# Storing x in the output and adding the gated product there by accumulating DMAs, in a hybrid-layer kernel on one core

## The chip, the cores and the metric

One core of a Trainium2 chip runs the whole kernel. The metric is the device time of one execution in microseconds; the time of a kernel is the median of its runs.

## The reference

One encoder layer over 2048 prompt tokens and 64 sample tokens (2112 in all), model width 1024, all in fp32. Cut to what matters here:

```python
proj = rms_norm(x, g_pre) @ w_in            # ten groups of 1024 columns
...                                         # path A: gated short convolution; path B: gated linear recurrence, 8 heads
merged = sigmoid(gA) * yA + sigmoid(gB) * yB
x = x + rms_norm(merged @ w_o, g_post)
gate = sigmoid(rms_norm(x, g_ple) @ w_ple_gate)
x = x + (p @ w_ple_proj) * gate             # the output y
```

The change concerns the last line: y is the sum of x (after the second last addition) and the product of the gate with what the text calls p, the projected per-layer embedding.

## The kernel before

The tokens are cut in three ranges ("blocks") of 768, 704 and 640. All data are feature-major: a tile is 128 features by the tokens of a range. Matrix products run in fp32 accuracy by splitting each operand into a high and a low part (three matmuls for each product, lines 388 to 390, 522 to 524 and 558 to 560), and in pairs of column groups by a seven-product scheme (Strassen and Winograd) over half-ranges. Weights come by DMA as tiles of 256 KB: the raw block (line 210), and, where it was computed earlier, its low part (line 232); ScalarE makes the high part (line 231, or 200 where the low part is computed anew on VectorE).

Each range goes through gates, heads (path B), convolution (path A), the merge with W_A and W_B, the product with W_O, a final norm, and the last gate with W_G. The order is written out by hand: generators are advanced at fixed places, `hooks` run one step after each group of matmuls, `paced` makes a POOL DMA wait for a given matmul, and `in_turn` walks over stages of seven steps (n = 0 to 6) with four groups (g = 0 to 3) each. The Tile scheduler then keeps the order of each engine and puts in the semaphores.

Where the last gate of each range is done:

- First range: its gate is a stage of the second range's merge, between W_A and W_B (`merge_in_turn`, `gate_in_turn`).
- Second range: its gate runs in the last range's time, as plain products (`final_gate`), while the last range's norm is done in hooks.
- Last range: its gate is the last stage of all (`gate_in_turn`).

For the first two ranges `final_norm` writes x (after the addition of the normed product) to a spill in HBM, `kept["x", j]` (lines 1225 and 1226), and the input of the gate to `kept["h2", j]`. The product p was written to `kept["p", j]` at the start. When the gate is done, x and p are read back: in the first range's gate `fetch` takes one ring tile for each of 16 half tiles (j, h), x in its left half and p in its right (lines 1161 to 1165), at the groups listed in `FETCH_AT`; in the second range's gate `final_gate` reads x and p for the next j ahead (line 1241, by `reload`, line 1126). Then ScalarE makes the sigmoid (lines 1273 and 1249), VectorE multiplies by p (1274 and 1250) and adds x (1275 and 1251), and the sum is stored to y: by POOL in the first range's gate (line 1277), by SP in the second's (line 1252).

Two pools of tiles matter: `ring` has 50 tiles of one range's width (`rt`), and `hf` has nine tiles of half a range (lines 132 and 133). A tile is given out again when all that read it are done, a store by DMA included. POOL issues its DMAs in order, and also does the power instruction of each norm (line 584).

Of the kernel before, what the change touches and what calls it, by code (L numbers as in the profile page):

```python
# [15 lines left out]
ALU = mybir.AluOpType  # L16
# [3 lines left out]
P = 128  # L20
D = 1024
KB = D // P
# [70 lines left out]
def hybrid_step(  # L93
# [17 lines left out]
    V, A, G, T, SP = nc.vector, nc.scalar, nc.gpsimd, nc.tensor, nc.sync  # L111
    blocks = plan()
# [16 lines left out]
    def rt(n=MAXN + 2, dt=F32):  # L129
        return ring.tile([P, MAXN + 2], dt, tag="r", name=nm("r"))[:, :n]  # L130
# [4 lines left out]
    def wide(x):  # L135
        return x.shape[1]
# [7 lines left out]
    def spill(kind, j, n):  # L144
        return dram.tile([P, MAXN], F32, tag=f"{kind}{j}", name=nm(kind), bufs=2)[:, :n]
# [106 lines left out]
    last, hooks, copies, adds = [None], [], [None], [None]  # L252
# [5 lines left out]
    def paced(dma):  # L258

        tc.add_manual_dep(  # L260
            dma.ins, last[0].name, mybir.DependencyInfo(mybir.DependencyClass.Sync, mybir.DependencyReason.DATA), reason="paced"
        )
# [156 lines left out]
    def half(t, h):  # L419
        n = wide(t) // 2  # L420
        return t[:, h * n : (h + 1) * n]
# [702 lines left out]
    def reload(d, pace=False):  # L1124
        t = rt(wide(d))
        dma = G.dma_start(t, d)
        if pace:
            paced(dma)
        return t

    def merge_in_turn(a, kept, mg, before):

        ob, m = [], []

        def gated(v, x, y):
            V.tensor_tensor(v, whole(x, y), v, ALU.mult)

        def sink_a(g, c, h, x, y):
            gated(half(m[g + c * KH], h), x, y)

        def sink_b(g, c, h, x, y):
            j = g + c * KH
            gated(half(mg[j], h), x, y)
            V.tensor_tensor(half(mg[j], h), half(mg[j], h), half(m[j], h), ALU.add)

        stages = [
            dict(idx=W_A, raw=a, sink=sink_a, anew=("A11", "A12")),
            dict(idx=W_B, raw=ob, sink=sink_b, anew=("A11", "A12")),
        ]
        plan = {(W_A, -1): (kept, GA, m), (W_A, 1): (kept, GA, m), (W_A, 6): (kept, GB, mg), (W_B, 1): (kept, GB, mg)}  # L1150
        if before is None:
            plan |= {(W_A, 3): (kept, "o", ob), (W_A, 5): (kept, "o", ob)}
            order = []
        else:
            rows, fetched = [], {}
            stages.insert(1, gate_in_turn(before[0], rows, lambda j, h: fetched.pop((j, h)), ("A11", "A12", "A22")))
            plan |= {(W_A, 3): (before[1], "h2", rows), (W_A, 5): (before[1], "h2", rows)}
            plan |= {(W_A, 4): (kept, "o", ob), (W_A, 6): (kept, "o", ob), (W_G, 6): (kept, GB, mg)}
            order = [(g + c * KH, h) for c, h in ((0, 0), (1, 0), (1, 1), (0, 1)) for g in range(KH)]

        def fetch(j, h):
            t = rt(before[0]["n"])
            for q, kind in enumerate("xp"):
                paced(G.dma_start(half(t, q), half(before[1][kind, j], h)))
            fetched[j, h] = half(t, 0), half(t, 1)

        def loads(idx, n, g=0, count=1):

            src, kind, tiles = plan.get((idx, n), (kept, None, m))
            if kind is not None:  # L1170
                tiles.extend(reload(src[kind, j], n >= 0) for j in range(len(tiles), len(tiles) + count))
            if idx == W_G and order and n * KH + g in FETCH_AT:
                fetch(*order.pop(0))

        return stages, loads
# [18 lines left out]
    def final_norm(bl, segs, xo, acc, h2, kept, raw=False):  # L1194


        c = slice(segs[0]["off"], segs[-1]["off"] + segs[-1]["n"])
        n = sum(sg["n"] for sg in segs)
        acc2, rs, rs2 = rt(bl["n"]), rt(bl["n"]), rt(bl["n"])
        xks = []  # L1200

        def fetch():
            j = len(xks)
            if j < KB:
                xks.append(rt(bl["n"]))
                G.dma_start(xks[j][:, c], x_fm[j * P : (j + 1) * P, segs[0]["t0"] : segs[0]["t0"] + n])

        fetch()
        copy = V.tensor_copy if bl["last"] else A.copy
        for _ in rms(acc, rs, segs, copy):  # L1210
            fetch()
            yield
        for j in range(KB):
            fetch()
            xj = xo[j][:, c]
            V.scalar_tensor_tensor(xj, xj, g_post[:, j : j + 1], rs[:, c], ALU.mult, ALU.mult)
            V.tensor_tensor(xj, xj, xks[j][:, c], ALU.add)
            for i in (j - 1,) if 0 < j < KB - 1 else (j - 1, j) if j else ():
                sum_squares(i, xo[i][:, c], acc2[:, c], n)
            yield  # L1220
        yield from rms(acc2, rs2, segs, copy)
        for j in range(KB):
            xj = xo[j][:, c]
            if kept is not None:
                kept["x", j] = spill("x", j, bl["n"])
                G.dma_start(kept["x", j], xo[j])
            if len(h2) <= j:
                h2.append(rt(bl["n"]) if raw else (rt(bl["n"], F32R), rt(bl["n"], F32R)))
            t = h2[j] if raw else rt(bl["n"])
            V.scalar_tensor_tensor(t[:, c], xj, g_ple[:, j : j + 1], rs2[:, c], ALU.mult, ALU.mult)  # L1230
            if not raw:
                split(t[:, c], h2[j][0][:, c], h2[j][1][:, c])
            elif kept is not None:
                kept["h2", j] = spill("h2", j, bl["n"])
                G.dma_start(kept["h2", j], t)
                h2[j] = None
            yield

    def final_gate(bl, segs, h2, kept, queue=G):
        def fetch(j):  # L1240
            return [reload(kept[kind, j]) for kind in "xp"] if j < KB else None

        nxt = fetch(0)
        for j in range(KB):
            pss = gemm(W_G + j, h2, segs)
            (xj, pj), nxt = nxt, fetch(j + 1)
            t = rt(bl["n"])
            for s, ps in zip(segs, pss):
                A.activation(t[:, cols_of(s)], ps, AF.Sigmoid)
            V.tensor_tensor(t, pj, t, ALU.mult)  # L1250
            V.tensor_tensor(t, t, xj, ALU.add)
            queue.dma_start(y_fm[j * P : (j + 1) * P, bl["t0"] : bl["t0"] + bl["n"]], t)
            yield

    def rows_again(kept, h2):
# [7 lines left out]
                split(lo.bitcast(F32), hi, lo)  # L1263
                yield

    def gate_in_turn(bl, h2, parts, anew=()):

        def sink(g, c, h, x, y):
            j = g + c * KH
            v = whole(x, y)  # L1270
            gate = hf(wide(v)) if y is None else v
            xj, pj = parts(j, h)
            A.activation(gate, v, AF.Sigmoid)  # L1273
            V.tensor_tensor(gate, gate, pj, ALU.mult)  # L1274
            V.tensor_tensor(gate, gate, xj, ALU.add)  # L1275
            o = bl["t0"] + h * wide(v)
            (SP if (c, h) == (0, 1) and bl["last"] else G).dma_start(y_fm[j * P : (j + 1) * P, o : o + wide(v)], gate)

        return dict(idx=W_G, raw=h2, sink=sink, anew=anew)

# [14 lines left out]
    kepts = [{} for _ in blocks]  # L1295
# [3 lines left out]
    with tc.high_priority():  # L1299
# [41 lines left out]
        ph, done = split_p(ph0)  # L1341
        with behind_all(done):
            done = [held_split(j) for j in range(2)][-1]
# [12 lines left out]
    for n, ks in enumerate(((0,), (1, 2), (3, 4), (5,), (6,), (7,))):  # L1356
        with behind_all(done):
            for k in ks:
                done = add_square(k)
        with placed():  # L1360
            run(first_ple, 1)
        with behind_all(done):
            done = held_split(n + 2)
    with behind_all((*done, *copies)):
        cols = [col_rstd(half(acc, h), n0 // 2) for h in range(2)]
        ph, done = split_p(ph1)
# [26 lines left out]
    for bi, bl in enumerate(blocks):  # L1393
# [57 lines left out]
        if nxt:  # L1451
            fills = gates(nxt, hc, kepts[bi + 1], False)
            norm = final_norm(bl, segs, xo, acc[0], h2, kept, True)
            spread_out((norm, (0, 1, 0, 0, 0, 1) + (0, 1, 0) * (KB - 1) + (0, 1) + (0, 0, 1, 0, 0, 0, 1) + (0, 1) * (KB - 3) + (1, 1, 1)))
            run(fills, LEAD)
            assert not hooks
        else:
            plans = (0, 2, 1, 1, 0, 1, 2, 2, 2, 2), (1, 0, 1, 1, 2, 1, 2, 2, 1, 0, 1, 2, 2, 2, 2)
            spread_out((norms[1], plans[1]), (norms[0], plans[0]))
            raws = load_p(bl, G)  # L1460
            for j, _ in enumerate(final_gate(blocks[bi - 1], blocks[bi - 1]["segs"], rows2, kepts[bi - 1], SP)):
                if j == 3:
                    ph = [split_rt(raw) for raw in raws]
            run(ple(bl, ph, kept))
            assert not hooks
            first_rows = [narrow(half(t, 0)) for t in h2[:KH]]
            run(in_turn([gate_in_turn(bl, h2, lambda j, h: (half(xo[j], h), half(kept["p", j], h)))], first_rows))
# [49 lines left out]
```

## Time and profile before

| | us |
|---|---|
| median of 3 runs | 2552.84 |
| lowest and highest run | 2550.76, 2552.87 |
| the profiled execution, its own time | 2552.61 |
| its span, first to last instruction | 2550.6 |
| VectorE, ScalarE, POOL busy | 1915.9, 1618.7, 421.3 |
| DMA moved | 693.54 MB, mean 272 GB/s |

A busy time is the sum over an engine's instructions in the span; DMA-issuing instructions are not counted on SP, but the time that POOL spends on issuing a DMA (about 0.54 us) is shown where its rows are listed. Rows of a stretch of time give, for each engine, busy us and the number of instructions, then the granted TensorE clock, the mean busy share of the 16 DMA engines and what they moved. A wait is shown as the waiting instruction, what ended the wait, the total, the number and the longest. Rows of single instructions have start and duration in us, the line, what is written and read, and in brackets how long the engine had been idle and what released it. Rows of a line give durations in ns (least, median, largest) and the first and last start. Rows of DMA issues give count, KB each and the median us to landing.

### The profile page before, as it was taken

How to read it: one execution, taken by the hardware profiler on the slowest of the kernel's cores; microseconds unless marked ns; L12 is line 12 of the kernel's file. 1: busy time of each engine (PE TensorE's matmuls, PEld its weight loads, DVE VectorE, ACT ScalarE, POOL GpSimd, SP SyncE). 2: the span in 40 equal slices, each digit the busy share in tenths (PEclk: the TensorE clock that was granted, in tenths of full speed). 3: DMA queues.
4: the chain of work that ended last, by engine and by line, in shares of the span. 5: the costliest groups of instructions: out<-in, count | busy, mean ns of one | idle time of the engine just before them, and what ended most of it. 6: DMA issues, size and time to landing. Idle time of an engine off the chain costs nothing. (4 is left out here: it accounts for less than half of the span.)

```text
span 2550.6 us, 47470 instructions
## 1 busy us (share of the span) xinstructions
PE 2534.3 (99%) x16198; PEld 2519.8 (99%) x16198; DVE 1915.9 (75%) x3714; ACT 1618.7 (63%) x3136; POOL 421.3 (17%) x774
## 2 busy tenths in 40 slices
PE   8999999999999999999999999999999999999999
PEld 8999999999999999999999999999999999999998
DVE  8788888899889867677755578986566655568966
ACT  6666666555465766777845466676677754456736
POOL 1012111222110021223221013102100010011221
PEclk9999999999999999999999999999999999999999
DMA  7678877898888797778777789989866667789977
GB/s 275 217 262 272 279 247 266 288 325 299 283 322 266 255 355 262 246 259 270 252 263 230 212 309 358 338 277 360 307 197 199 196 209 235 234 288 338 312 262 250
DMA packets 330290, 693.54 MB, mean 272 GB/s; under 512 B 41632, under 2 KB 46272, under 8 KB 330048
## 3 DMA queue, kind: packets, MB, share of 16 engines
q1 hardware_dynamic: 283392, 513.73, 60.8%
q0 software_dynamic: 46368, 176.74, 19.2%
q8 instruction: 127, 2.08, 0.3%
q14 instruction: 115, 0.94, 0.1%
q10 hardware_dynamic: 288, 0.05, 0.0%
HBM read 507.10 MB, written 183.26 MB: 271 GB/s over the span
## 5 line engine op out<-in xcount | busy, mean ns | idle before, releaser
L388 PE MATMUL pg<-r,hi 128*128 128x320 f32 (+2 forms) x3304 | 1086.7, 329 | 0.0
L389 PE MATMUL pg<-r,hi 128*128 128x320 f32 (+2 forms) x3304 | 1065.9, 323 | 0.0
L390 PE MATMUL pg<-r,lo 128*128 128x384 f32 (+2 forms) x2056 | 673.0, 327 | 0.0
L388 PEld LDWEIGHTS pg<-r,hi 128*128 128x128 f32 x3304 | 621.6, 188 | 0.4
L389 PEld LDWEIGHTS pg<-r,hi 128*128 128x128 f32 x3304 | 621.4, 188 | 0.0
L231 ACT CAST hi<-raw 128x512 fp32r<-128x512 f32 x544 | 335.3, 619 | 319.2 <-PE pg L389 133.9
L200 ACT CAST hi<-raw 128x512 fp32r<-128x512 f32 x454 | 280.9, 620 | 279.3 <-PE pg L389 132.5
L200 DVE TENSOR_TENSOR lo<-raw,hi 128x512 fp32r<-128x512 f32 x454 | 312.0, 688 | 154.3 <-ACT hi L200 126.1
L523 PE MATMUL pg<-r,hi 128*128 128x384 f32 (+2 forms) x1232 | 398.1, 325 | 1.1 <-DVE r L200 0.6
L390 PE MATMUL pg<-r,s 128*128 128x320 f32 (+1 forms) x1248 | 393.9, 316 | 0.1
L522 PE MATMUL pg<-r,hi 128*128 128x384 f32 (+2 forms) x1232 | 388.2, 325 | 1.1 <-ACT r L200 1.1
L390 PEld LDWEIGHTS pg<-r,lo 128*128 128x128 f32 x2056 | 386.2, 188 | 0.0
L200 DVE TENSOR_TENSOR r<-r,r 128x320 fp32r<-128x320 f32 (+6 forms) x426 | 246.4, 596 | 66.4 <-ACT r L200 64.0
L524 PE MATMUL pg<-r,lo 128*128 128x384 f32 (+2 forms) x800 | 257.8, 324 | 0.9 <-DMA lo<-low 0.9
L523 PEld LDWEIGHTS pg<-r,hi 128*128 128x128 f32 x1232 | 231.3, 188 | 5.9 <-DVE r L200 4.7
L200 ACT CAST r<-r 128x320 fp32r<-128x320 f32 (+6 forms) x426 | 221.0, 547 | 24.9 <-DVE r L369 16.2
L390 PEld LDWEIGHTS pg<-r,s 128*128 128x128 f32 x1248 | 234.4, 188 | 0.3 <-DMA s<-low 0.3
L522 PEld LDWEIGHTS pg<-r,hi 128*128 128x128 f32 x1232 | 228.5, 188 | 5.7 <-ACT r L200 5.0
L200 ACT CAST hi<-s 128x512 fp32r<-128x512 f32 x160 | 98.7, 617 | 113.1 <-PE pg L389 102.5
L402 ACT COPY hf<-pg 128x352 f32<-128x352 f32 (+2 forms) x354 | 156.0, 444 | 10.5 <-PE pg L390 10.3
L524 PEld LDWEIGHTS pg<-r,lo 128*128 128x128 f32 x800 | 150.2, 188 | 1.6 <-DMA lo<-low 1.5
L524 PE MATMUL pg<-r,s 128*128 128x320 f32 (+2 forms) x432 | 139.1, 322 | 0.0
(370 smaller groups left out, 3720.3 us busy)
## 6 DMA issues: line engine op xcount, KB each, us to landing
raw<-w_blk SPq DMA_DIRECT2D x550, 256.0 KB, 4.0
raw<-S SPq DMA_DIRECT2D x488, 256.0 KB, 3.8
s<-low SPq DMA_DIRECT2D x428, 256.0 KB, 3.9
low<-lo SPq DMA_DIRECT2D x178, 256.0 KB, 3.3
S<-s SPq DMA_DIRECT2D x152, 256.0 KB, 3.4
lo<-low SPq DMA_DIRECT2D x116, 256.0 KB, 5.0
low<-r POOLq DMA_DIRECT2D x88, 256.0 KB, 4.8
r<-w_blk POOLq DMA_DIRECT2D x72, 256.0 KB, 7.1
```

The costliest lines, as they stand in the source:

```text
L200: return A.copy(hi, src).ins, V.tensor_tensor(lo, src, hi.bitcast(F32), ALU.subtract).ins
L231: A.copy(hi, raw)
L388: add(hi[:, k, :], xhi, start=start and k == 0, stop=False)
L389: add(hi[:, k, :], xlo, start=False, stop=False)
L390: last[0] = add(lo[:, k, :], xhi, start=False, stop=k == KH - 1).ins
L402: copied = A.copy(got[n], ps[bank])
L522: add(hi[:, k, :], xhi, start=start and k == 0, stop=False)
L523: add(hi[:, k, :], xlo, start=False, stop=False)
L524: last[0] = add(lo[:, k, :], xhi, start=False, stop=k == KH - 1).ins
```

## The change

`final_norm` stores x of the first two ranges straight into y by a plain DMA on POOL (it wrote the spill before) and keeps that instruction. In the two gates p alone is requested: in the first range's gate two halves share one ring tile. The gate times p is then added to y in HBM by an accumulating DMA from POOL (`add_to_y`), which has a semaphore wait on the store of x. The additions on VectorE and the reads of x go; the second range's stores move from SP to POOL. The last range's gate is as before.

```diff
+    def add_to_y(bl, kept, j, o, t):
+
+        done = G.dma_start(y_fm[j * P : (j + 1) * P, bl["t0"] + o : bl["t0"] + o + wide(t)], t, accum_op=ALU.add)
+        tc.add_manual_dep(
+            done.ins, kept["y", j].name, mybir.DependencyInfo(mybir.DependencyClass.Sync, mybir.DependencyReason.DATA), reason="x in y"
+        )
+
     def merge_in_turn(a, kept, mg, before):
...
-            rows, fetched = [], {}
-            stages.insert(1, gate_in_turn(before[0], rows, lambda j, h: fetched.pop((j, h)), ("A11", "A12", "A22")))
+            rows, fetched, shared = [], {}, [None]
+            stages.insert(1, gate_in_turn(before[0], rows, lambda j, h: (None, fetched.pop((j, h))), ("A11", "A12", "A22"), before[1]))
...
         def fetch(j, h):
-            t = rt(before[0]["n"])
-            for q, kind in enumerate("xp"):
-                paced(G.dma_start(half(t, q), half(before[1][kind, j], h)))
-            fetched[j, h] = half(t, 0), half(t, 1)
+            if j % 2 == 0:
+                shared[0] = rt(before[0]["n"])
+            fetched[j, h] = half(shared[0], j % 2)
+            paced(G.dma_start(fetched[j, h], half(before[1]["p", j], h)))
...
             if kept is not None:
-                kept["x", j] = spill("x", j, bl["n"])
-                G.dma_start(kept["x", j], xo[j])
+                kept["y", j] = G.dma_start(y_fm[j * P : (j + 1) * P, bl["t0"] : bl["t0"] + bl["n"]], xo[j]).ins
...
-    def final_gate(bl, segs, h2, kept, queue=G):
+    def final_gate(bl, segs, h2, kept):
         def fetch(j):
-            return [reload(kept[kind, j]) for kind in "xp"] if j < KB else None
+            return reload(kept["p", j]) if j < KB else None
...
-            (xj, pj), nxt = nxt, fetch(j + 1)
+            pj, nxt = nxt, fetch(j + 1)
...
             V.tensor_tensor(t, pj, t, ALU.mult)
-            V.tensor_tensor(t, t, xj, ALU.add)
-            queue.dma_start(y_fm[j * P : (j + 1) * P, bl["t0"] : bl["t0"] + bl["n"]], t)
+            add_to_y(bl, kept, j, 0, t)
...
-    def gate_in_turn(bl, h2, parts, anew=()):
+    def gate_in_turn(bl, h2, parts, anew=(), kept=None):
...
             V.tensor_tensor(gate, gate, pj, ALU.mult)
+            if kept is not None:
+                add_to_y(bl, kept, j, h * wide(v), gate)
+                return
             V.tensor_tensor(gate, gate, xj, ALU.add)
...
```

More of the change, by code (lines that the diff above doesn't have):

```diff
@@ L1274, in sink @@
             V.tensor_tensor(gate, gate, pj, ALU.mult)
+            if kept is not None:
+                add_to_y(bl, kept, j, h * wide(v), gate)
+                return
             V.tensor_tensor(gate, gate, xj, ALU.add)
             o = bl["t0"] + h * wide(v)
-            (SP if (c, h) == (0, 1) and bl["last"] else G).dma_start(y_fm[j * P : (j + 1) * P, o : o + wide(v)], gate)
+            (SP if (c, h) == (0, 1) else G).dma_start(y_fm[j * P : (j + 1) * P, o : o + wide(v)], gate)
         return dict(idx=W_G, raw=h2, sink=sink, anew=anew)
@@ L1460, in hybrid_step @@
             raws = load_p(bl, G)
-            for j, _ in enumerate(final_gate(blocks[bi - 1], blocks[bi - 1]["segs"], rows2, kepts[bi - 1], SP)):
+            for j, _ in enumerate(final_gate(blocks[bi - 1], blocks[bi - 1]["segs"], rows2, kepts[bi - 1])):
                 if j == 3:
```

## The prediction

> **What bounds the kernel now.** I read the page's busy times first, then the waits of TensorE, then the busy time by stage around the places the change touches. All terms below are made against the profiled execution, 2552.61 us, whose span is 2550.6 us; 2.0 us lie around the span. The median of the three runs shown, 2552.84, is 0.2 us above it and the lowest run 1.9 us below, so 0.2% (5.1 us) is about what a measurement can tell from no change.
>
> ```profile
> span 2550.6 us, 47470 instructions
> PE 2534.3 (99%) x16198; PEld 2519.8 (99%) x16198; DVE 1915.9 (75%) x3714; ACT 1618.7 (63%) x3136; POOL 421.3 (17%) x774
> ...
> 6.87 0.69 PE L1103 MATMUL pa<-r,r 128*128 128x384 f32 x1 [6.87 <-ACT r L200]
> ...
> 2544.58 0.31 PE L524 MATMUL pg<-r,lo 128*128 128x320 f32 x1
> ...
> PE pa L1103 <- ACT r L200: 6.9, 1, 6.9
> PE pg L522 <- ACT r L200: 1.1, 1, 1.1
> PE pg L524 <- DMA lo<-low: 0.9, 1, 0.9
> PE pg L523 <- DVE r L200: 0.6, 1, 0.6
> PE pg L459 <- ACT r L767: 0.3, 1, 0.3
> PE pa L1105 <- DVE r L200: 0.2, 1, 0.2
> ```
>
> TensorE is idle for 2550.6 - 2534.3 = 16.3 us only. 6.9 us are the wait for the first input, which nothing here moves. The last matmul starts at 2544.58 and takes 0.31, so 5.7 us follow it (the last gate, its add and its store). Three waits, 1.1 + 0.9 + 0.6 = 2.6 us, remain as something a change in the middle could take away. The next view says where they lie: busy time of each engine in five stretches, then the DMA share and GB/s.
>
> ```profile
> 1543.00:1568.00 25.00, 24.37 (x137) 23.26 (x136) 22.32 (x47) 15.46 (x31) 7.00 (x14) 1.00 0.95 341
> 1568.00:1600.00 32.00, 31.98 (x183) 31.44 (x182) 25.49 (x51) 22.03 (x48) 16.55 (x31) 1.00 1.00 362
> 1600.00:1620.00 20.00, 18.93 (x113) 18.21 (x112) 18.43 (x39) 12.83 (x27) 7.46 (x14) 1.00 1.02 385
> 1620.00:1640.00 20.00, 19.11 (x118) 18.62 (x116) 15.90 (x36) 11.51 (x26) 0.60 (x2) 1.00 0.87 289
> 2414.00:2484.00 70.00, 70.00 (x446) 69.86 (x445) 48.88 (x98) 28.60 (x63) 16.21 (x27) 1.00 0.78 277
> ```
>
> From 1543 to 1620 us runs the gate of the first token range inside the second range's merge (here called the gate stage), and all three waits lie in it or just behind. Its DMA engines are full: 0.95 x 25 + 1.00 x 32 + 1.02 x 20 = 76.2 of 77 us. From 2414 to 2484 the second range's gate runs (the late gate): 78% of DMA, and TensorE never stops. The waits one by one:
>
> ```profile
> 1554.86 0.44 PE L523 MATMUL pg<-r,hi 128*128 128x384 f32 x1 [0.63 <-DVE r L200]
> ...
> 1611.88 0.62 ACT L200 CAST hi<-raw 128x512 fp32r<-128x512 f32 x1 [1.83 <-DMA raw<-w_blk]
> ...
> 1613.29 0.59 PE L522 MATMUL pg<-r,hi 128*128 128x352 f32 x2 [1.07 <-ACT r L200]
> ...
> 1625.79 0.43 PE L524 MATMUL pg<-r,lo 128*128 128x352 f32 x1 [0.89 <-DMA lo<-low]
> ```
>
> The wait at 1613 names ScalarE, but ScalarE had itself stood 1.83 us for a weight; the one at 1625 is a weight's low part. So two of the three (2.0 us) are DMA being late, and the one at 1554 is VectorE, ahead of any add that the change removes. **What decides is therefore DMA time in the gate stage**, not the instructions saved.
>
> **The change part by part.**
>
> ```profile
> L1164 POOL DMA_DIRECT2D r<-x x12: 536/536/550, 1568.0 to 1594.1; - x12
> ...
> L1277 POOL DMA_DIRECT2D y_fm<-hf x16: 539/544/549, 1559.8 to 1612.2; - x16
> ...
> L1277 POOL DMA_DIRECT2D y_fm<-hf x7: 539/544/544, 1583.8 to 1598.6; - x7
> ...
> L1277 POOL DMA_DIRECT2D y_fm<-hf x5: 539/539/544, 1602.7 to 1612.2; - x5
> ...
> q0 software_dynamic: 3823, 12.72, 43.9%
> ...
> r<-x POOLq DMA_DIRECT2D x16, 192.0 KB, 5.5
> ...
> y_fm<-hf POOLq DMA_DIRECT2D x16, 192.0 KB, 5.7
> ...
> y_fm<-hf SPq DMA_DIRECT2D x4, 160.0 KB, 1.8
> ```
>
> (The queue row and the two transfer rows under it are of 1543 to 1620 us alone; the last row is of the kernel's end.) It gives the price of a byte: 43.9% of 77 us is 33.8 us for 12.72 MB, 2.66 us per MB on all 16 engines. A 192 KB transfer (0.197 MB) is 0.52 us of DMA time.
>
> 1. *The x reloads of the gate stage go*: 16 x 0.52 = 8.4 us of DMA time, 16 x 0.54 = 8.6 us of POOL's issuing. The p requests stay, with their pacing, two halves in one tile now. POOL loses only work; its free time between issues is idle already (16.55 of 32 us busy in the fullest stretch), so this half gives nothing.
>
> 2. *The 16 stores of the gate stage become accumulating ones.* Nothing of before shows such a transfer. From below it is a plain store, 0.52 us and 5.7 us to landing. The nearest rows above are the pair it replaces: one x read and one y store move the same bytes over the same engines, 1.04 us, with 5.5 + 5.7 = 11.2 us if one must land before the other. Farther off: if every engine also stood for the shortest store's landing (1.8 us, the last row), 2.84 us each. I take 1.04, because the addend in y must still be fetched from HBM and the sum written: the same read and write, no longer by two instructions. Then DMA time comes out as 16 x 1.04 - 16 x 0.52 - 16 x 0.52 = 0. Ends: -8.4 us and +16 x 1.8 = +29 us.
>
> The Trainium skill, "Collectives: The Full Stack", section "The bandwidth ceiling: the fold count and why AG ≠ RS ≠ AR", speaks against hoping for the low end: an adding transfer is held to half a copy's rate not by the add but by its two source reads on one ring. By that the 16 cost 16.6 us instead of 8.4 and the sum is again 0; no run here shows it yet.
>
> 3. *Where the DMA time falls moves.* Of the 16 x reads four lie before 1568 and 12 in 1568 to 1600; of the stores 4, 7 and 5 in the three stretches. At 1.04 each: 0 before 1568, (7 - 12) x 0.52 = -2.6 us in the second stretch, +5 x 0.52 = +2.6 us in the third, which is the one at 1.02 where weights are late now. What it costs TensorE lies between 0 (the relief just before carries over) and 2.6 us; I take 1.0.
>
> 4. *Adds go.* 16 in the gate stage, 8 in the late gate:
>
> ```profile
> 1558.38 0.56 DVE L1275 TENSOR_TENSOR hf<-hf,r 128x384 f32<-128x384 f32 x1
> ...
> L1251 DVE TENSOR_TENSOR r<-r,r x8: 883/888/894, 2428.0 to 2482.2; 128x704 f32<-128x704 f32 x8
> ```
>
> 16 x 0.56 = 9.0 us and 8 x 0.89 = 7.1 us of VectorE. In the third stretch VectorE is 92% busy (18.43 of 20), so operands for the next stage get ready sooner by up to the 5 adds there, 2.8 us; but the stops there wait for weights. I credit 0.5 us. In the late gate TensorE does not wait, so 0.
>
> 5. *The late gate.* 8 x reads go, 8 stores move from SP to POOL and accumulate.
>
> ```profile
> r<-x POOLq DMA_DIRECT2D x8, 352.0 KB, 6.4
> ...
> L1252 SPq EVENT_SEMAPHORE  x8: 17/2018/2612, 2426.4 to 2483.2; - x8
> L1252 SPq DMA_DIRECT2D y_fm<-r x8: 337/338/655, 2428.9 to 2483.2; - x8
> ...
> 2457.95 0.89 DVE L1250 TENSOR_TENSOR r<-r,r 128x704 f32<-128x704 f32 x1 [3.74 <-ACT r L1249]
> ...
> 2465.76 0.89 DVE L1250 TENSOR_TENSOR r<-r,r 128x704 f32<-128x704 f32 x1 [0.19 <-ACT r L1249]
> ```
>
> SP no longer stands some 2.0 us per store ahead of weight requests: worth 0, since no weight is late there. POOL gets 8 issues of 0.54 us in place of 8 reads of 0.54 us, and now waits for the multiply of line 1250; queued behind it is the p request two groups on, whose multiply comes 2 x 7.8 us later and whose data land in about 6 us, and the norm's power instructions, which follow the same multiply on VectorE anyway. DMA: 0 at the pair's price; if each cost 2.84 us per 192 KB, 8 x 1.8 x 352/192 = 26 us more against 0.22 x 70 = 15 us free, only there could it show. Cover: the free 15 us.
>
> 6. *The x spills (lines 1225 and 1226) become plain stores into y*, 16 of the same size on the same queue: 0. *The new wait for them* is on POOL; they were issued hundreds of microseconds before: 0.
>
> ```profile
> L1226 POOL DMA_DIRECT2D x<-r x16: 539/539/547, 898.1 to 1767.1; - x16
> ```
>
> 7. *Staging tiles.* A gate half (pool hf, nine deep) is held until its store lands. The second store of its group at 1586.46 lands about 5.7 us later; the ninth tile after it is written at 1595.71:
>
> ```profile
> 1586.46 0.54 POOL L1277 DMA_DIRECT2D y_fm<-hf  x1
> ...
> 1595.71 0.47 ACT L544 COPY hf<-pg 128x384 f32<-128x384 f32 x1
> ```
>
> The slack is 3.5 us, so landings up to 9.2 us hide behind it; past that a ScalarE copy, with weight casts queued behind it and TensorE behind those, is late.
>
> Sum: 0 (DMA total) + 1.0 (its place) - 0.5 (VectorE) = +0.5 us: 2553.1 us.
>
> **The rivals.** (a) *The accumulate costs as a plain store.* The stage then has 8.4 us of free DMA, the two weight waits go (-2.0), all three at best (-2.6): 2550.0 to 2550.6. For it: no row excludes it. Against: the bytes of y must be read. Still within 0.2%; a gain over 5.1 us would need more idle time than the 2.6 us there is. (b) *The accumulate makes a third pass*: read, add, write with the engine held, 3 x 0.52 = 1.56 us. 16 x 0.52 = 8.4 us more DMA time where 0.8 of 77 us are free, so TensorE waits for weights about 7.6 us more, from 1583 on: 2560.2. It decides for slower from (5.1 + 0.8)/16 + 1.04 = 1.4 us each. For it: the stage is full, and the landing of weights there is already long:
>
> ```profile
> raw<-S SPq DMA_DIRECT2D x23, 256.0 KB, 7.3
> raw<-w_blk SPq DMA_DIRECT2D x14, 256.0 KB, 10.1
> ```
>
> Against: relief of the x reads just ahead. (c) *Long landing at a fair price*: engine time 1.04, but 11.2 us or more to landing; the tiles of step 7 come 2 us late each, four stores in a row of them, 2 to 8 us on TensorE: 2558. Against: the ninth-tile slack begins at the stores of 1583 only, and ScalarE works ahead. (d) *It is hidden altogether*, -0.5 to 0: the same as the forecast's own range.
>
> **How the numbers follow.** Forecast with (d) 0.65, (a) 0.12, (b) and dearer 0.14, (c) 0.05, something that gains over 5.1 us and that I do not see 0.04. Forecast, (d) and (a) are within 0.2%: 0.77. Slower 0.14 + 0.05 = 0.19, faster 0.04. The likeliest's own range is 2551.5 to 2555.5. The range asked for goes down to (a) less the runs' scatter, 2549.3, and up to (b), 2560.5; what is left out is the dearer part of (b), and the gain.
>
> **What would show it.** Right: no x rows at lines of the fetch, DMA share from 1568 to 1600 a little under 1.00 and from 1600 to 1620 still full, the weight waits near 1613 and 1625 there and up to 1 us longer, the late gate at 70 of 70 us. Rival (a): those two waits gone, GB/s down. Rival (b): more "DMA" waits of TensorE between 1583 and 1640, the gate stage some 7 us longer. Rival (c): waits of ScalarE or VectorE for a DMA into y ahead of tile hf. It would be wrong as a whole if the tail behind the last matmul (5.7 us) changed, which no step touches.

## The result, and the profile after

| | before | changed |
|---|---|---|
| median of 22 runs, us | 2552.27 | 2557.3 |
| ratio, 95% interval | | 1.0018, 1.0011 to 1.0024 |
| profiled execution, its own time (span), us | 2552.61 (2550.6) | 2558.56 (2556.9) |
| VectorE busy, us (instructions) | 1915.9 (3714) | 1902.1 (3690) |

The changed kernel is slower by 0.18%, some 4.6 us, clear of no difference but within the 0.2% that the prediction called no change. In a second measurement it was 1.0018 again (1.0009 to 1.0027). One of the 22 runs of the changed kernel took 14296 us; the ratio leaves it out, and nothing on record says where that time went.

The waits of TensorE in the profile after (total, number, longest):

```profile
PE pa L1103 <- ACT r L200: 6.9, 1, 6.9
PE pg L524 <- DMA lo<-low: 3.4, 1, 3.4
PE pg L390 <- DMA s<-low: 1.0, 2, 0.8
PE pg L522 <- ACT r L200: 0.9, 2, 0.8
PE pg L523 <- DVE r L200: 0.4, 1, 0.4
```

The wait for a weight's low part (line 524) has grown from 0.9 to 3.4 us. The same stretches as before, busy times of each engine, granted clock, DMA share and GB/s, and then the place of the stop (where TensorE stands), first after, then before:

```profile
1543.00:1568.00 25.00, 24.65 (x140) 23.93 (x140) 21.49 (x45) 16.55 (x34) 7.28 (x11) 1.00 1.01 315
1568.00:1600.00 32.00, 32.00 (x184) 32.00 (x183) 22.50 (x45) 21.33 (x46) 12.41 (x19) 1.00 0.97 303
1600.00:1620.00 20.00, 19.10 (x115) 18.50 (x114) 18.69 (x41) 12.11 (x27) 8.54 (x13) 1.00 1.09 329
1620.00:1640.00 20.00, 16.62 (x88) 16.34 (x87) 12.31 (x27) 8.80 (x19) 0.54 (x1) 0.83 0.88 308
...
1621.00:1625.60 4.60, 1.33 (x9) 1.04 (x7) 3.40 (x8) 2.94 (x7) 0.40 (x1) 0.87 1.04 397
1625.60:1632.20 6.60, 6.50 (x25) 6.50 (x26) 2.54 (x4) 1.20 (x2) 0.00 (x0) 0.57 0.76 262
...
1625.70 0.66 PE L524 MATMUL pg<-r,lo 128*128 128x352 f32 x1 [3.38 <-DMA lo<-low]
```
```profile
1621.00:1625.60 4.60, 3.90 (x25) 3.61 (x23) 4.60 (x12) 1.11 (x2) 0.54 (x1) 1.00 0.96 334
1625.60:1632.20 6.60, 6.41 (x40) 6.41 (x40) 5.78 (x12) 4.61 (x10) 0.00 (x0) 1.00 0.70 253
```

Two things cost time here. TensorE stands 3.4 us for the low part. And behind the stop the granted clock is 0.57: from 1625.60 to 1632.20, 25 matmuls run where 40 ran before. Fifteen matmuls at 0.165 us (6.60 us by 40) are 2.5 us that no row of waits shows. Of the profile's 6.3 us more span, the waits give 5.7 - 2.6 = 3.1 us (the head's aside) and the clock behind the stop 2.5. Each profile is one execution, and the stop is not the same in all of them: how far it varies is shown with the experiments.

The accumulating transfers themselves, at line 1133 (POOL's issue in ns), and the POOL queue from 1543 to 1620 us:

```profile
L1133 POOL DMA_DIRECT2D y_fm<-hf x16: 844/868/1049, 1558.6 to 1607.9; - x16
...
q0 software_dynamic: 4108, 9.73, 46.1%
...
y_fm<-hf POOLq DMA_DIRECT2D x16, 192.0 KB, 7.2
```

The queue's time is 46.1% of 77 us = 35.5 us. The 16 accumulating transfers are 3.15 MB of it. Its plain part, 9.73 - 3.15 = 6.58 MB at the 2.66 us per MB of before, is 17.5 us; the remaining 18.0 us are the 16 transfers, 1.12 us each or 2.1 times a plain store. What in them takes the time the trace does not show. Over the whole span the changed kernel and the one with plain stores (below) move the same 687.51 MB, so no read of the addend is counted; what differs is the number of packets, 329906 against 328114, with 2048 more under 2 KB, which is 128 for each of the 16 transfers.

### The profile page after: what moved, and what is told of

It reads as the page before. It is cut to its first block, busy times and chain, and to the rows that moved or that the text cites. A ratio compares the mean times of both kernels' runs of the same rounds, so it can differ in the third digit from the quotient of the medians.

```text
span 2556.9 us, 47389 instructions
## 1 busy us (share of the span) xinstructions
PE 2537.6 (99%) x16198; PEld 2524.2 (99%) x16198; DVE 1902.1 (74%) x3690; ACT 1618.7 (63%) x3136; POOL 422.8 (17%) x758
## 2 busy tenths in 40 slices
DMA packets 329906, 687.51 MB, mean 269 GB/s; under 512 B 41248, under 2 KB 47936, under 8 KB 329664
```

## The experiments

Times are medians of 11 runs (of 8 in the last row); each ratio is to the kernel before on the same chip. The four rows with "plain" leave x out of part of y, so they are measures and not candidates.

| kernel | us | ratio, 95% interval |
|---|---|---|
| changed, again | 2556.96 | 1.0018, 1.0009 to 1.0027 |
| plain stores | 2550.18 | 0.9992, 0.9983 to 1.0001 |
| gate stage only | 2557.36 | 1.0016, 1.0007 to 1.0025 |
| late gate only | 2553.20 | 1.0002, 0.9993 to 1.0010 |
| last eight plain | 2549.17 | 0.9990, 0.9981 to 0.9999 |
| first eight plain | 2552.52 | 1.0003, 0.9994 to 1.0012 |
| x read back from y | 2553.66 | 1.0007, 0.9999 to 1.0016 |
| last eight deferred | 2555.85 | 1.0017, 1.0008 to 1.0025 |
| changed, S2 low computed | 2551.88 | 0.9994, 0.9985 to 1.0003 |
| before, S2 low computed | 2553.55 | 1.0003, 0.9994 to 1.0012 |
| plain stores, POOL copies | 2557.35 | 1.0019, 1.0011 to 1.0028 |
| before with two stops | 2557.11 | 1.0016, 1.0006 to 1.0026 |

**Is it the accumulating, and where?** Four kernels: the changed one again,

> The changed kernel once more, as the measure for the others on this chip. Theory A (place of the DMA time: an accumulating 192 KB transfer takes twice a plain store's engine time, the last eight fall where the DMA engines are full, a weight's low part comes late near 1622 us and the long stop halves the granted clock for some 7 us): 3 to 6 us above the kernel before, with a wait of TensorE for a low part of 2 to 4 us near 1622. Theory B (POOL: 0.87 us for an issue in place of 0.54 delays what is queued behind it), C (x stored into y is slower than into the spill) and D (the late gate) expect the same total and differ in the kernels below.

plain stores in its place,

```diff
-, t, accum_op=ALU.add)
+, t)
```

> The changed kernel with plain stores in place of the accumulating ones: x is left out of y for the first two ranges. A: the gate stage has 8 to 10 us less DMA time than the changed kernel, the wait near 1622 goes, no halved clock there; 2549 to 2551.5, at or below the kernel before. B: also faster, since plain issues take 0.54 us. C: stays 3 to 6 us above the kernel before. D: falls to the kernel before.

accumulating in the gate stage alone (the second range's `final_gate`, spill and SP store from the kernel before),

> Accumulating only in the gate stage of the first range; the second range's spill, reload, add and SP store are as before. A: all of the loss stays, 2555 to 2558. D: back to the kernel before, 2552. C: about half of the loss, the stop near 1752 gone.

and accumulating in the late gate alone (the first range from the kernel before).

> Accumulating only in the late gate of the second range; the first range as before. A and B: as the kernel before within 1.5 us, TensorE without a stop from 2414 to 2484. D: the whole loss, 2556. C: about half of it, with a stop near 1752.

With plain stores the loss is gone; the gate stage alone has all of it, the late gate alone none that can be measured. D falls. The profile with plain stores at the same place:

```profile
1600.00:1620.00 20.00, 20.00 (x123) 19.64 (x122) 19.74 (x43) 12.86 (x28) 7.01 (x14) 1.00 1.02 368
1620.00:1640.00 20.00, 20.00 (x126) 19.99 (x126) 15.97 (x34) 14.73 (x32) 0.01 (x1) 1.00 0.97 333
```

TensorE never stops there and the clock is whole. The saving of 8 to 10 us of DMA time that theory A expected does not show as such: from 1543 to 1620 the share fell from 1.01 to 0.96, 4 us, and 25.68 MB were moved in place of 24.13. The DMA share from 1620 to 1640 is 0.97, so the 0.87 of the kernel before, where TensorE stood 0.9 us, is no measure of free room.

The stop near 1622 is not the changed kernel's alone. The kernel that accumulates in the late gate only, whose gate stage is as before, has it too, and so has the one further down that reads x back from y and accumulates nowhere. In this order, the wait and the stretch it lies in:

```profile
PE pg L524 <- DMA lo<-low: 2.1, 1, 2.1
...
1620.00:1640.00 20.00, 17.88 (x101) 17.42 (x99) 13.45 (x30) 9.23 (x21) 0.54 (x1) 0.91 0.75 261
```
```profile
PE pg L524 <- DMA lo<-low: 2.8, 1, 2.8
...
1620.00:1640.00 20.00, 17.19 (x96) 16.73 (x96) 12.76 (x29) 8.78 (x20) 0.40 (x1) 0.91 0.70 251
```

So with the old gate stage the wait for the low part was 0.9, 2.1 and 2.8 us in these profiles and 0.7 us in that of the two forced stops (last row of the table); with accumulating in it, 3.4, 4.3 (the changed kernel again) and 4.8 (gate stage only), and the clock of the stretch was 0.83 in all three. The accumulating lengthens a stop that was there; the pair 0.9 and 3.4 alone shows too much of it.

**Which of the sixteen?**

```diff
+        plain = dict() if bl["t0"] == 0 and o else dict(accum_op=ALU.add)      # last eight; "not o" for the first eight
-, t, accum_op=ALU.add)
+, t, **plain)
```

> The changed kernel with plain stores for the last eight of the sixteen products of the gate stage (x left out of y there); the first eight and the late gate accumulate. A by place: most of the loss goes, 2550.5 to 2553, no wait over 1.5 us near 1622 and full clock. Rival A' (the total of DMA time counts, wherever it falls): half of the loss, 2554 to 2555.

> The mirror: plain stores for the first eight (x left out there), accumulating for the last eight and the late gate. A by place: most of the loss stays, 2555 to 2557.5, with the wait near 1622. A': half of it, 2554 to 2555.

Both sizes were missed: 2549.2 and 2552.5, each below both theories. The two halves do not add up. Against its own kernel before, plain stores alone are at -2.1 us, accumulating in the first eight alone -2.9, in the last eight alone +0.5, in all +4.6. The stretches 1568 to 1600, 1600 to 1620 and the one after, of the two kernels in this order, and the stop of the second:

```profile
1568.00:1600.00 32.00, 32.00 (x185) 32.00 (x184) 22.50 (x45) 21.32 (x47) 11.62 (x19) 1.00 0.98 316
1600.00:1620.00 20.00, 20.00 (x122) 19.64 (x122) 19.75 (x43) 12.78 (x28) 7.00 (x13) 1.00 1.03 385
1620.00:1640.00 20.00, 20.00 (x126) 19.99 (x125) 16.02 (x34) 14.71 (x32) 0.00 (x0) 1.00 0.97 334
```
```profile
1568.00:1600.00 32.00, 32.00 (x184) 32.00 (x183) 22.06 (x44) 22.40 (x48) 10.42 (x18) 1.00 0.91 303
1600.00:1620.00 20.00, 20.00 (x121) 19.65 (x120) 19.75 (x43) 13.40 (x30) 9.83 (x14) 1.00 1.08 316
1620.00:1640.00 20.00, 17.82 (x101) 17.54 (x100) 13.47 (x29) 9.65 (x21) 1.08 (x2) 0.91 0.95 341
...
1625.61 0.43 PE L524 MATMUL pg<-r,lo 128*128 128x352 f32 x1 [2.17 <-DMA lo<-low]
```

Of the two, only the kernel that accumulates in the last eight has the stop. With the stretch ahead of them at 0.91, where the kernels that accumulate in all sixteen have 0.97 to 1.00, the stop is 2.2 us, not 3.4 to 4.8. (This profile is of a run of 2556.49 us, 4 us above its kernel's median.) So a plain sum of DMA time does not give the loss: two kernels with eight accumulating transfers each in the gate stage are 3.4 us apart by their place, and the time asked for just ahead seems to count as well.

**Is the store of x into y slow (C)?**

> x stored into y by the norm as in the changed kernel, but read back from y and added on VectorE, and the sum stored plainly: no accumulating transfer. C (the store into y is slow): 1.5 us or more above the kernel before, with a stop near 1752. A, B: within 1 us of the kernel before.

1.0007, with no wait near 1752, and the stop of 2.8 us near 1622 that was shown above: C is not supported, though up to 0.16% is not excluded.

**Deferring the last eight.** The product is written into p's tile, and the transfer is paced in the W_B stage.

```diff
+            if kept is not None and h:
+                V.tensor_tensor(pj, gate, pj, ALU.mult)
+                deferred.append((bl, kept, j, h * wide(v), pj))
...
+            if idx == W_B and deferred and n * KH + g in LATER_AT:       # 10, 12, ... 24
+                paced(add_to_y(*deferred.pop(0)))
```

> The whole change, but the last eight products are written into p's tile and their accumulating transfers are issued one by one in the W_B stage behind, from its third step on, where 11 to 13% of the DMA time was free. A by place: the wait near 1622 shrinks to what it was before or less, 2550.5 to 2553. A': as the changed kernel, 2555 to 2557. A cost that it could show: p's tiles are held some 25 us longer.

It missed: 2555.85. The stop near 1622 did go, but a new one came (ScalarE, and TensorE behind it; line numbers shifted by 3):

```profile
1639.20 0.48 ACT L203 CAST r<-r 128x352 fp32r<-128x352 f32 x1 [4.73 <-DMA y_fm<-r]
...
1639.74 0.42 PE L525 MATMUL pg<-r,hi 128*128 128x352 f32 x1 [1.30 <-ACT r L203]
1641.62 0.66 PE L525 MATMUL pg<-r,hi 128*128 128x352 f32 x1 [0.74 <-ACT r L203]
...
1643.00:1648.00 5.00, 5.00 (x19) 5.00 (x19) 3.70 (x8) 2.28 (x5) 0.85 (x1) 0.52 0.79 198
```

ScalarE waits 4.7 us for a deferred transfer: the row names a ring tile still being added to y. Behind the waits of TensorE that follow from it the granted clock is 0.52 for 5 us: 19 matmuls run where some 30 fit at 0.165 us, about 1.9 us more. The kernel's total therefore says nothing for or against place; its cost is the one named as possible. (The profiled run, 2559.03 us, is the slowest of its eleven.)

**Less DMA asked for at that place.** In the second range's W_B the low part of S2 (one of the sums of weight blocks in the seven-product scheme) is computed, not read: four transfers of 256 KB less.

```diff
-        return split_w(load_raw(sums[i1][name]), (i1, name), low=low)
+        return split_w(load_raw(sums[i1][name]), None if anew else (i1, name), low=low)
...
-            dict(idx=W_B, raw=ob, sink=sink_b, anew=("A11", "A12")),
+            dict(idx=W_B, raw=ob, sink=sink_b, anew=("A11", "A12") if before is None else ("A11", "A12", "S2")),
```

> The whole change, and in the second range's W_B stage the low part of S2 is computed on VectorE (four times about 0.69 us) instead of read from HBM: four 256 KB transfers, some 2.8 us of DMA time, less right where the low part comes late near 1622. Theory A'' (what counts is the DMA time asked for in the stretch that ends at the stop, about 1590 to 1622, against what the weights need there; moving it behind the stop only moves the stop): the stop near 1622 goes or falls under 2 us and the clock stays whole, 2550 to 2553.5. Rival E (the stop belongs to the accumulating transfers' slow landing, whatever else is asked for): unchanged, 2556 to 2557.5.

> The same edit on the kernel before, as its control: A'': 0.5 to 2 us below the kernel before (its own stop there is 1 to 3 us from run to run). E: no difference. If it ends below the first kernel of this call, the change has no gain left even where its loss is taken away.

The loss goes: 0.9994 instead of 1.0018, with all accumulating transfers in place; E falls. The profile:

```profile
L1133 POOL DMA_DIRECT2D y_fm<-hf x16: 842/868/1052, 1561.5 to 1610.7; - x16
...
1600.00:1620.00 20.00, 20.00 (x121) 19.64 (x120) 19.86 (x42) 13.17 (x28) 9.78 (x14) 1.00 1.09 322
1620.00:1640.00 20.00, 19.68 (x122) 19.15 (x120) 16.91 (x37) 12.14 (x27) 1.07 (x2) 1.00 0.89 319
...
PE pg L390 <- DMA s<-low: 1.8, 1, 1.8
```

No stop near 1622, and the clock is whole there. POOL's issues are as long as in the changed kernel, so by themselves they do not make the loss (theory B). The expected gain of the same edit on the kernel before did not come (1.0003): its profile has no wait for a low part either, but 1.5 us for ScalarE and 1.2 us for VectorE instead. Neither version is below the kernel before by more than its interval. The last row is a stop at 1750 us, discussed at the end; the profiled run, 2555.81 us, is the slowest of its eleven, so the median may hold less of it.

**POOL's longer issue (B), by itself.**

```diff
-, t, accum_op=ALU.add)
+, t)
...
+        G.tensor_copy(tmp, omlb)
+        G.tensor_copy(tmp, omlb)
```

> The changed kernel with plain stores (x left out of y for the first two ranges), and after each of them two small copies on POOL, 0.37 us, so that POOL is held about as long (0.91 us) as by an accumulating issue (0.87 us). B (POOL's longer issue is the loss): 2555 to 2557. A and A'': as with plain stores alone, 2549.5 to 2551.5.

This one did not test what it was meant for. Nothing held the copies in place: they ran at the kernel's start, from 6 us on, and TensorE stood there for POOL's power instruction:

```profile
PE pa L595 <- POOL cols L584: 4.6, 1, 4.6
...
20.00:29.00 9.00, 5.86 (x38) 5.54 (x37) 4.03 (x8) 4.79 (x10) 7.50 (x21) 1.00 0.64 232
29.00:36.00 7.00, 5.58 (x19) 5.25 (x20) 3.56 (x5) 2.93 (x6) 3.28 (x5) 0.51 0.84 324
```

It shows another thing: a stop of 4.6 us far from the gate stage, and a clock of 0.51 in the 7 us from 29 us on.

**Does a stop lower the clock by itself?** The kernel before, with two waits of TensorE for POOL in the first range's W_O stage:

```diff
+            done = G.tensor_tensor(held_up, held_up, mhalf.to_broadcast([P, 3]), ALU.pow)      # once; three times
...
+                    if k == 0 and gate is not None:
+                        tc.add_manual_dep(
+                            mm.ins, gate.name, mybir.DependencyInfo(mybir.DependencyClass.Sync, mybir.DependencyReason.DATA), reason="stop"
+                        )
```

> The kernel before with two forced stops of TensorE in the first range's W_O stage: one waits for one power instruction on POOL, the other for three in a row (about 1.5 us each). If a long stop itself lowers the clock: the short one (some 2 us) is followed by full or by 3.4 us of half clock, the long one (4 to 5 us) by 6.8 us of half clock, and the total rises by the stops and half of these stretches, 9 to 12 us. If the half clock seen near 1624 comes from DMA load instead: full clock behind both, and a rise of 6 to 7 us.

```profile
849.00:851.00 2.00, 0.97 (x6) 0.65 (x5) 1.40 (x3) 1.87 (x5) 0.89 (x1) 1.00 0.93 331
851.00:855.00 4.00, 4.00 (x25) 4.00 (x24) 2.28 (x4) 3.07 (x7) 0.00 (x0) 1.00 0.86 260
867.00:871.00 4.00, 1.24 (x8) 0.92 (x6) 3.26 (x7) 2.39 (x6) 3.01 (x3) 1.00 1.01 384
871.00:875.00 4.00, 3.98 (x14) 3.98 (x15) 0.00 (x0) 0.55 (x2) 0.00 (x0) 0.58 0.06 22
875.00:879.00 4.00, 4.00 (x25) 4.00 (x24) 3.05 (x6) 2.77 (x7) 0.00 (x0) 0.99 0.38 133
```

Behind 1.0 us of waiting 25 matmuls run in 4 us at full clock. Behind 2.8 us the clock is 0.58 for 4 us and 14 matmuls run, with the DMA engines nearly idle. Both stops came out shorter than planned, so the rise, 4.1 us, is below the 9 to 12 expected; that a long stop lowers the clock, and that the slow clock needs no DMA load while it lasts, is shown. During both waits the DMA engines were busy (0.93 and 1.01).

## Why the prediction was right, and where it was not

The time lies in the range, and the change is within 0.2% as forecast, but by little: the interval reaches 0.24%, and 2557.3 is 4.2 us above the 2553.1 given and outside the likeliest's own range (to 2555.5). The forecast had the cost hidden. It was not, and that the loss stayed under 0.2% is in part luck. Nor is 0.2% what a measurement can tell from no change: 22 runs told 0.18% from none.

- What bounds: right. DMA in the gate stage decided, and the instructions saved did not make up for it (24 adds went, VectorE lost 13.8 us of work).
- Step 2, the price: 1.04 us taken, 1.12 measured, so rival (a) and rival (b) both fall. The reason given, that the addend is fetched from HBM, stays an argument: the bytes counted do not show it, and smaller packets are a rival that no run tested. The Trainium skill, "Collectives: The Full Stack", section "The bandwidth ceiling: the fold count and why AG ≠ RS ≠ AR", puts the half rate of an adding ring transfer down to its two source reads; the factor agrees here, 2.1, the reason is not shown. In the late gate it was dearer than step 5 had it, 2.4 times a plain transfer by the same working (47.6% of 70 us for the POOL queue's 8.00 MB, at the 2.74 us per MB of before for the plain part): DMA share 0.84 from 2420 to 2490 in place of 0.78 from 2414 to 2484, still hidden (70.00 of 70 us busy). Rival (a)'s time, 2550.0 to 2550.6, is what plain stores gave (2550.18).
- Step 3, the place, is the term that was mis-sized. The five transfers from 1600 on did raise that stretch from 1.02 to 1.09, but TensorE got the upper end: 2.5 us more for the low part where 1.0 was put down (in this pair of profiles; the old gate stage had 0.7 to 2.8 us in four). The relief ahead of it was not there in full: from 1568 to 1600 the share fell by 0.03 of 32 us, 1.0 us where 2.6 were put down, and before 1568, put at 0, it rose from 0.95 to 1.01.
- Missing altogether: the clock behind the stop, 2.5 us in the profile. The sum had each microsecond of waiting at one microsecond. This term and step 3 together are most of the 4 us that the forecast is off.
- Step 5: the issue of an accumulating transfer on POOL was taken at 0.54 us; it is 0.87 in the gate stage. It cost nothing that shows. Step 7: landing 7.2 us, within the 9.2; rival (c) did not come. Step 6: nothing that can be told from zero.

## What to carry to other kernels

Adding in HBM saved no DMA time here: an accumulating transfer held the engines 1.12 us, a reload and a store together 1.04, and all of it falls at the time of the store, while a reload could have come earlier. Where DMA is full, look at when each transfer falls and at what the weights need next, not at the total; a stretch that looks less than full behind a stop may be the stop's own shadow. Count a stop of TensorE of some 2 us or more at its length and half of the slow stretch behind it, and look for the same behind several short waits close together. And take more than one profile before a wait in it is called what a change made: the same wait was 0.7 to 2.8 us with the old gate stage.

## What the runs showed of the hardware that had not been expected

The granted clock after a stop goes in steps. Read in windows of 1 us, it is 0.50 in each slow stretch named here, and the stretch has one of two lengths. It was 3.4 us long with single waits of 1.85 to 2.8 us (five profiles: S2's low part computed, late gate only, first eight plain, x read back, the forced stop), and 6.8 us with 3.4 to 4.8 us (four: the changed kernel twice, gate stage only, POOL copies). In the long ones part of it lies within the wait: in the changed kernel the slow stretch runs from 1624.4 to 1631.2, and the wait ended at 1625.7. Single waits of 0.9 to 1.4 us left the clock whole. But one wait's length does not decide alone: in the deferred kernel waits of 1.3, 0.7 and 0.3 us within 4.1 us also brought 6.8 us at 0.50. Three kinds of single stops lowered the clock: for weights, for POOL at the head, and the forced one. The shortest of them, in the kernel with S2's low part computed (0.57 is the mean of 3.4 us at 0.50 and the rest at full clock):

```profile
1750.08 0.41 PE L390 MATMUL pg<-r,s 128*128 128x320 f32 x1 [1.85 <-DMA s<-low]
...
1751.00:1755.00 4.00, 4.00 (x19) 4.00 (x18) 1.99 (x4) 2.14 (x5) 0.00 (x0) 0.57 0.99 371
```

The Trainium skill, "TensorE: Matmul & The Clock Gate", section "Why this matters for your kernels", warns of idle gaps above about 3 us. Here 1.85 us of waiting was enough, and the measurement decides.

What stays open is this stop at 1748 to 1758 us itself (a low part late in the last range's gates; 0.8 us in the profile of the changed kernel). At 0.4 to 1.8 us it shows in five of the kernels that accumulate in the gate stage, also where the second range's x goes to a spill, and not in the profile before; no run was made for it. Nor was POOL's longer issue tried by itself in the gate stage, nor an accumulating transfer with fewer, larger packets.
